# A streaming-encoder block with 32 experts: fillers placed around the routing, the tail in a planned order

## The chip, the cores and the metric

The kernel runs on one core of a Trainium2 chip. The metric is the time of one execution in microseconds (us), as a median over runs; one execution was profiled as well. The engines are named as in the profile: PE (TensorE, its weight loads PEld), DVE (VectorE), ACT (ScalarE), POOL (GpSimd) and SP, which issues most DMAs. Each engine takes its instructions in the order in which they are written.

## What is computed

For 1024 tokens of 1024 numbers, all in fp32:

```python
h = rmsnorm(x, g_mix); z = h @ w_in
x = x + concat(conv_branch(z), lru_branch(z)) @ w_out
hf = rmsnorm(x, g_ffn)
eid, gate = hier_route(hf)        # top 1 of 4 groups, then top 2 of its 8 experts
x = x + sum over the 2 chosen experts of gate * ((silu(hf @ w1[e]) * (hf @ w3[e])) @ w2[e])
e = rmsnorm(p @ w_ple, g_ple_proj)                  # p: 1024 x 256
pg = sigmoid(rmsnorm(x, g_ple) @ w_ple_gate)        # w_ple_gate: 1024 x 1024
out = rmsnorm(x + pg * e, g_final)
```

w1 and w3 are 1024 x 512 for each of 32 experts, w2 is 512 x 1024.

## The kernel before

Every fp32 matrix product is made of three fast passes on PE: each operand is split into a high part (`split_hi`, L235, a copy on ACT) and a low part (`split_lo`, L238, a subtraction on DVE, for some tiles on POOL), and high x high, high x low and low x high are summed in PSUM (`mmr`, L244). Tokens are worked in NT = 8 tiles of 128 rows.

**Front.** The code up to the routing is written as small generators (`c_...`) that a list planner, the class `Flow`, puts in order: each step names its engine, a cost and a lag, takes buffers from counted pools ("s": 36 slots of 128 x 1024) and waits for marks; among the steps that could start soonest the one of lowest rank goes first. The order that comes out is the order of the instructions, and the tile framework adds the semaphores. `c_mix` adds the mixer's output for a tile and makes hf, which goes to DRAM (hf_d); `c_router` makes the logits; `c_route` runs twice (tiles 0 to 4, then 5 to 7) and chooses experts with some 60 small DVE steps, rank matmuls (rk) and table matmuls (stab, L1083); `c_tables` reads the table into toki (the token of each row of an expert), dsti and gat. `c_ple` makes p @ w_ple for the first NPG = 5 tiles as filler work for PE, and keeps or stores (e_d) its result. `c_usplit` splits the first unit of expert weights.

**Experts.** A unit is 1 MB of one expert's weights, loaded as two slots: four units of w1/w3 (`up`) and two of w2 (`down`) for each expert, 192 in all; the list `units` puts the next expert's first two ahead of an expert's down units. Loads run AHEAD = 13 units before their use, splits SL = 2 units before. Behind the routing come the first gather of token rows (`gather`, L1349, an indirect DMA on POOL, index toki), the branch for experts with more than 128 tokens (`overflow`, L1423, not taken here) and then the loop over units. An expert's product goes silu and multiplication (`act_mul`, L1383 and L1384), transposes (hTp), a split, the down product (tile ey), a scaling by the gate (ys, L1526) and a scatter into y_d (L1354).

**Tail.** From `mctx.close()` on the framework's own scheduler orders the instructions. p for the last tiles is transposed and split, w_ple is split, `ple(i)` makes tiles 5 to 7. `load_wg` and `split_wg` bring w_ple_gate; five of its eight low parts are made on POOL (WGP). For each tile `post_norm` adds the two rows of y_d (yy) that the experts gave (L1630), squares, takes the root (`rs_of`, L287, pow on POOL), multiplies by it and g_ple (L1637) and transposes (xgT); `post_mm` makes the 48 gate matmuls (pg, for some tiles in the buffer named ey); `post_out` makes sigmoid (L1663), product with e (L1664), sum (L1665), square (L1666), root, and the last product with g_final (L1672), and stores. The last tile does this in two halves of 512 columns.

## Time and profile before

| | |
|---|---|
| median of 3 runs | 1087.73 us (1086.04 to 1088.53) |
| the profiled execution | 1087.43 us, span 1085.7 us, mean granted PE clock 0.984 |
| busy in the span | PE 1021.4 (94%), DVE 931.0 (86%), PEld 838.6 (77%), ACT 727.3 (67%), POOL 281.9 (26%) |
| DMA | 281.49 MB, mean 259 GB/s |

The span is the time from the first to the last recorded instruction or transfer; 1.7 us of the execution's time lie around it. In a timeline a row is start, duration, engine, line, operation and tiles; the bracket at its end is the idle time of the engine in front of it and what ended that. The granted clock is a share of PE's 2.4 GHz; 0.5 is 1.2 GHz.

### The profile page before, as it was taken

How to read it: one execution, taken by the hardware profiler on the slowest of the kernel's cores; microseconds unless marked ns; L12 is line 12 of the kernel's file. 1: busy time of each engine (PE TensorE's matmuls, PEld its weight loads, DVE VectorE, ACT ScalarE, POOL GpSimd, SP SyncE). 2: the span in 40 equal slices, each digit the busy share in tenths (PEclk: the TensorE clock that was granted, in tenths of full speed). 3: DMA queues.
4: the chain of work that ended last, by engine and by line, in shares of the span. 5: the costliest groups of instructions: out<-in, count | busy, mean ns of one | idle time of the engine just before them, and what ended most of it. 6: DMA issues, size and time to landing. Idle time of an engine off the chain costs nothing. (4 is left out here: it accounts for less than half of the span.)

```text
span 1085.7 us, 14177 instructions
## 1 busy us (share of the span) xinstructions
PE 1021.4 (94%) x4839; PEld 838.6 (77%) x4840; DVE 931.0 (86%) x1109; ACT 727.3 (67%) x932; POOL 281.9 (26%) x235
## 2 busy tenths in 40 slices
PE   4999999979999799999999999999999999867995
PEld 4887768758888688888888888888888888655884
DVE  5999999999556699999999999999999999669863
ACT  5447878772333688888888888888787888643331
POOL 6459576631210210111111111111010100033110
PEclk9999999999999899999999999999999999979998
DMA  9310002243326889999999999999999999477511
GB/s 270 99 39 20 19 20 78 96 155 118 117 97 207 311 315 405 400 403 401 381 395 391 381 402 385 388 392 385 382 385 382 385 379 394 154 275 290 174 40 58
DMA packets 101070, 281.49 MB, mean 259 GB/s; under 512 B 16849, under 2 KB 34945, under 8 KB 100993
## 3 DMA queue, kind: packets, MB, share of 16 engines
q1 hardware_dynamic: 89216, 255.79, 63.2%
q0 software_dynamic: 10592, 21.01, 5.2%
q10 hardware_dynamic: 1184, 3.75, 0.9%
q8 instruction: 39, 0.64, 0.2%
q14 instruction: 39, 0.31, 0.1%
HBM read 265.28 MB, written 31.98 MB: 274 GB/s over the span
## 5 line engine op out<-in xcount | busy, mean ns | idle before, releaser
L1349 POOL DMA_INDIRECT xg<-hf_d,toki x32 | 43.8, 1370 | 361.0 <-PE xgT L295 348.6
L549 DVE SCALAR_TENSOR_TENSOR fir<-u,V,fir 128x512 f32<-128x512 f32 (+20 forms) x180 | 133.2, 743 | 5.0
L235 ACT ACTIVATE xTh<-xgT 128x512 fp32r<-128x512 f32 x80 | 47.1, 598 | 77.3 <-PE xgT L295 77.3
L584 POOL TENSOR_TENSOR acc<-fpr,acc 128x512 f32<-128x512 f32 x60 | 86.2, 1437 | 40.6 <-ACT fpr L574 37.6
L1354 POOL DMA_INDIRECT y_d<-ys,dsti x32 | 39.1, 1220 | 147.9 <-ACT ys L1526 147.9
L287 POOL TENSOR_TENSOR rs<-ms,mhalf 128x1 f32<-128x1 f32 x32 | 23.2, 727 | 155.2 <-DVE ms L281 155.2
L238 DVE TENSOR_TENSOR xTl<-xgT,xTh 128x512 fp32r<-128x512 f32 x80 | 54.4, 686 | 6.8 <-ACT xTh L235 6.8
L244 PE MATMUL zvg<-hTh,whi 128*128 128x512 f32 (+1 forms) x144 | 56.7, 394 | 0.0
L244 PE MATMUL zvg<-hTh,wlo 128*128 128x512 f32 (+1 forms) x144 | 53.2, 369 | 0.0
L244 PE MATMUL zvg<-hTl,whi 128*128 128x512 f32 (+1 forms) x144 | 53.0, 368 | 0.0
L574 ACT ACTIVATE fpr<-u,V 128x512 f32<-128x512 f32 x60 | 41.9, 717 | 15.4 <-POOL acc L584 15.3
L295 PE MATMUL xgT<-ident,xg 128*128 128x128 f32 x256 | 38.8, 276 | 7.0 <-DVEq L1423 7.0
L295 PEld LDWEIGHTS xgT<-ident,xg 128*128 128x128 f32 x256 | 32.2, 142 | 14.9 <-issue 7.1
L1526 ACT ACTIVATE ys<-ey,gat 128x1024 f32<-128x1024 f32 x32 | 35.4, 1107 | 7.1 <-PE ey L244 7.1
L244 PE MATMUL wo<-wohi,lnyhl 128*128 128x512 f32 x128 | 39.4, 404 | 0.7 <-DVE lnyhl L238 0.7
L238 POOL TENSOR_TENSOR wlo<-wraw,whi 128x1024 fp32r<-128x1024 f32 x14 | 34.3, 2453 | 20.2 <-ACT whi L235 20.2
L1383 ACT ACTIVATE silu<-eab 128x512 f32<-128x512 f32 x32 | 19.2, 599 | 29.0 <-PE eab L244 29.0
L855 ACT ACTIVATE hf<-xre 128x1024 f32<-128x1024 f32 x8 | 8.5, 1058 | 42.0 <-DVE xre L843 33.4
L244 PE MATMUL pg<-wglo,xTh 128*128 128x512 f32 x96 | 32.0, 401 | 3.6 <-POOL wglo L238 2.3
L244 PE MATMUL pg<-wghi,xTl 128*128 128x512 f32 x96 | 31.7, 398 | 1.5 <-DVE xTl L238 1.5
L244 PE MATMUL pg<-wghi,xTh 128*128 128x512 f32 x96 | 32.4, 404 | 0.2 <-ACT xTh L235 0.2
L244 PEld LDWEIGHTS zvg<-hTl,whi 128*128 128x128 f32 x144 | 27.7, 192 | 5.8 <-issue 1.7
(3324 smaller groups left out, 3514.3 us busy)
## 6 DMA issues: line engine op xcount, KB each, us to landing
wraw<-in_w_in_dram SPq DMA_DIRECT2D x16, 512.0 KB, 5.1
yy<-y_d SPq DMA_DIRECT2D x16, 512.0 KB, 5.1
xin<-in_x_dram SPq DMA_DIRECT2D x8, 512.0 KB, 7.1
woraw<-in_w_out_dram SPq DMA_DIRECT2D x8, 512.0 KB, 3.7
xre<-in_x_dram SPq DMA_DIRECT2D x8, 512.0 KB, 4.1
hf_d<-hf POOLq DMA_DIRECT2D x8, 512.0 KB, 5.2
x2r<-x_d SPq DMA_DIRECT2D x8, 512.0 KB, 8.0
wgraw<-in_w_ple_gate_dram SPq DMA_DIRECT2D x8, 512.0 KB, 6.1
```

What stands on the lines that cost most here:

```text
L235: act.activation(r_(hi), src, AF.Copy)
L238: (eng or dve).tensor_tensor(out=r_(lo), in0=src, in1=hi, op=ALU.subtract)
L244: pe.matmul(out=o, lhsT=r_(l), rhs=r_(r), start=start, stop=stop)
L287: pool.tensor_tensor(out=rs, in0=ms, in1=mhalf[:, 0:1], op=ALU.pow)
L295: pe.transpose(out=t[:, k * P:(k + 1) * P], in_=src[:, off + k * P:off + (k + 1) * P], identity=ident)
L549: dve.scalar_tensor_tensor(f[:, a0 - t0:512], u[c][:, a0 - s:t1 - s], tap(c, s), f[:, a0 - t0:512], op0=ALU.mult, op1=ALU.add)
L574: act.activation(pr, u[c][:, 512 - s:1024 - s], AF.Copy, scale=tap(c, s))
L584: pool.tensor_tensor(out=a[:, 512:1024], in0=fprs.pop((c, s)), in1=a[:, 512:1024], op=ALU.add)
L1349: return pool.indirect_dma_start(out=dst, out_offset=None, in_=hf_d, in_offset=bass.IndirectOffsetOnAxis(ap=idx, axis=0), bounds_check=S - ...
L1354: return pool.indirect_dma_start(out=y_d, out_offset=bass.IndirectOffsetOnAxis(ap=idx, axis=0), in_=src, in_offset=None, bounds_check=2 * ...
L1383: act.activation(s_, w[:, 0:512], AF.Silu)
L1526: i = act.activation(ys, yw.pop(e), AF.Copy, scale=gat[:, e:e + 1])
```

## The change

It has three parts. At the routing, NPG is 4 instead of 5, the third and fourth ple tile wait for the marks "rk" and "slots" inside the routing, five units are loaded early instead of seven and a sixth right behind the first gather, the high parts of units 0 and 1 are made in the front, and the count for the branch is made ahead of the low parts. `c_mix` takes the mean of squares on POOL. In the tail, the last two units leave the loop and everything behind them is planned by a second `Flow`; w_ple_gate's raw blocks, p and half of w_ple come in during the last units; w_ple_gate is multiplied by g_ple when it is split, so that the raw sum is transposed and its root goes into the sigmoid's scale (rsx). The last tile's columns are cut into 512, 256 and 256, and its root is taken with ACT's Sqrt and DVE's reciprocal, with a small Sqrt (`c_table`) placed ahead of it. Removed with the old tail are `ple`, `e_load`, `split_wg`, `post_load`, `load_y`, `post_norm`, `post_mm` and `post_out`.

```diff
-EARLY = (3, 4, 5, 6, 7, 8, 9)
-PN0 = 6
-NPG = 5
-WGP = (1, 2, 3, 4, 5)
-PLU = 0
-PLW = 0
-WG0 = 2
-WG1 = 5
+EARLY = 5
+MORE = 6
+NPG = 4
+OFF2 = {}
+RK2 = {"pT": -30, "wp": -29, "wg": 0, "e": 12, "ple": -5, "xrs": 2}
...
@@ c_mix @@
-        yield go("DVE", 0.15)
-        ms = ms_of(ss, D)
-        yield go("POOL", 0.55)
-        rs = rs_of(ms)
+        yield go("POOL", 0.85)
+        rs = rs_of(ms_of(ss, D, pool))
...
+            order(load(x2_d[rows(i), :], xt), hfd[0], True)
...
@@ c_ple @@
+        if i == 3:
+            yield on("rk")
...
+            if i >= 2 and k == 1:
+                yield on("rk" if i == 2 else "slots")
...
+    def c_usplit(s):
+        yield on(("unit", s))
         yield get("s", 4)
         for j in range(2):
             yield go("ACT", 1.05)
             hi, lo = slot("ehi"), slot("elo")
...
+            split_hi(hi, raws[s][j])
+            his.setdefault(s, []).append((hi, lo))
...
@@ behind fl.run() @@
+    def early_lo(s, j):
+        split_lo(his[s][j][1], raws[s][j], his[s][j][0])
+        if j == 1:
+            raws.pop(s)
...
     g0 = gather(xg[0], toki[:, 0:1])
     pool.memset(gmark, 0.0)
     xg.append(bcp.tile([P, D], F32, name="xg1", tag="b"))
     pool.memset(xg[1], 0.0)
+    dve.tensor_reduce(cmx, cnt_f, op=ALU.max, axis=AX.X)
+    dve.tensor_copy(cmi, cmx)
+    for s in range(EARLY, MORE):
+        load_unit(s)
     for n, i in enumerate(ers):
         d = load(e_d[rows(i), :], ers[i])
         if n == 0:
             order(d, g0, True)
     ers.clear()
-    for s in range(len(EARLY), AHEAD):
-        load_unit(s, g0 if s == len(EARLY) else None)
-    dve.tensor_reduce(cmx, cnt_f, op=ALU.max, axis=AX.X)
-    dve.tensor_copy(cmi, cmx)
+    for s in range(MORE, AHEAD):
+        load_unit(s)
+    early_lo(0, 0)
+    early_lo(0, 1)
+    overflow()
+    early_lo(1, 0)
+    for j in range(1, NXG):
+        gather(xg[j], toki[:, j:j + 1])
+    xTs = {0: gather_T(xg[0])}
+    early_lo(1, 1)
...
@@ the loop over units @@
+    for s, (e, g) in enumerate(units[:-2]):
+        past = s + AHEAD - len(units)
+        if past == 0:
+            pt = p_load(1)
+        elif past == 1:
+            pw = {k: wp_load(k) for k in range(2)}
+        elif past > 2 and len(wgr) < 8:
+            load_wg(len(wgr))
...
+        if past in (8, 9):
+            k = past - 8
+            t = p_tr(pt, k)
             o = slot("phl")
             split_hi(o[:, 0:512], t)
             split_lo(o[:, 512:1024], t, o[:, 0:512])
-            pl[0][j, k], pl[1][j, k] = o[:, 0:512], o[:, 512:1024]
-    for k in range(2):
+            pl[0][1, k], pl[1][1, k] = o[:, 0:512], o[:, 512:1024]
+        elif past == 10:
+            k = 0
+            hi, lo = slot("wphi"), slot("wplo")
+            split_hi(hi, pw[k])
+            split_lo(lo, pw[k], hi)
+            pl[2][k] = hi, lo
...
+    def c_last():
+        e = NE - 1
+        yield get("m2")
+        yield go("ACT", 0.75, set="silu")
+        w = abw.pop(e)
+        s_ = m2("silu")
+        act.activation(s_, w[:, 0:512], AF.Silu)
+        yield go("DVE", 0.69)
+        dve.tensor_tensor(out=s_, in0=w[:, 512:1024], in1=s_, op=ALU.mult)
+        yield put("wp")
+        yield get("tp")
+        yield go("PE", 0.45, lag=0.35)
+        t = act_tr(s_)
+        yield put("m2")
+        yield get("m2", 2)
+        hi, lo = m2("hhi"), m2("hlo")
+        yield go("ACT", 0.6)
+        split_hi(hi, t)
+        yield go("DVE", 0.69)
+        split_lo(lo, t, hi)
+        yield put("tp")
+        yield get("yp")
+        w = None
+        for j in range(4):
+            yield go("PE", 6 * MM, lag=0.35 if j == 3 else 0.0)
+            w = w or ytile()
+            y_mm(w, (hi, lo), j, his[len(units) - 2 + j // 2][j % 2])
+            if j == 3:
+                yield put("m2", 2)
+            yield put("s", 2)
+        yield get("m4")
+        yl = m4("ys")
+        yield ("fork", -90, c_half(w, yl))
+        yield go("ACT", 0.6)
+        act.activation(yl[:, 0:512], w[:, 0:512], AF.Copy, scale=gat[:, e:e + 1])
+        yield on("ys1")
+        yield put("yp")
+        yield go("POOL", 1.1, lag=4.5)
+        put_rows(yl, e)
+        yield put("m4")
+        yield mark("sc")
+    def c_half(w, ys):
+        yield go("DVE", 0.69)
+        dve.tensor_scalar(ys[:, 512:1024], w[:, 512:1024], gat[:, NE - 1:NE], None, op0=ALU.mult)
+        yield mark("ys1")
...
+    def c_wps():
+        yield get("s", 2)
+        yield go("ACT", 1.05)
         hi, lo = slot("wphi"), slot("wplo")
-        split_hi(hi, pw[k])
-        split_lo(lo, pw[k], hi)
-        pl[2][k] = hi, lo
-    esq = slot("esq")
-    xs, es_, ei, yys, xTp, pgw = {}, {}, {}, {}, {}, {}
-    def ple(i):
-        w = wtile("ple") if i % 3 < 2 else ytile()
-        ple_mm(w, i, pl)
+        split_hi(hi, pw[1])
+        yield go("DVE", 1.22)
+        split_lo(lo, pw[1], hi)
+        pl[2][1] = hi, lo
+        yield put("s")
+        yield mark("pw")
...
+    def c_ple2(i):
+        yield get("wp")
+        w = None
+        for k in range(2):
+            if k:
+                yield on("pw")
+            for si in range(3):
+                yield go("PE", 2 * MM, lag=0.35 if k and si == 2 else 0.0)
+                w = w or wtile("ple")
+                ple_mm(w, i, pl, [(k, si)])
+        yield get("s")
+        es_[i] = slot("er")
+        yield ("fork", -1, c_esq(i, w))
+        yield on("gp")
+        yield go("DVE", 1.22)
+        dve.tensor_tensor(out=es_[i], in0=w, in1=gpb, op=ALU.mult)
+        yield on(("eq", i))
+        yield put("wp")
+        yield mark(("e", i))
...
+    def c_wg(k):
+        yield get("s", 2)
+        yield go("ACT", 1.05)
         hi, lo = slot("wghi"), slot("wglo")
-        split_hi(hi, raw)
-        split_lo(lo, raw, hi, pool if k in WGP else dve)
-        wg[k] = (hi, lo)
-    def post_load(i):
+        act.activation(r_(hi), wgr[k], AF.Copy, scale=vec("g_ple", k))
+        yield go("DVE", 1.22, port=True)
+        dve.scalar_tensor_tensor(r_(lo), wgr[k], vec("g_ple", k), hi, op0=ALU.mult, op1=ALU.subtract)
+        yield put("s")
+        wgs[k] = (hi, lo)
+        yield mark(("wg", k))
...
+    def c_y(i):
+        yield on("sc")
+        if i >= 2:
+            yield on(("xt", i - 2))
+        if i:
+            yield on(("yl", i - 1))
+        yield get("s", 2)
+        ys[i] = slot("y0"), slot("y1")
+        cuts = (0, 512, D) if i == 0 else (0, D)
+        for c, (a, b) in enumerate(zip(cuts, cuts[1:])):
+            f = (b - a) / D
+            for k in range(2):
+                yield go("SP", 1.35 * f, lag=0.0)
+                q = load(ys[i][k][:, a:b], y_d[k * S + i * P:k * S + (i + 1) * P, a:b])
+                for sc in scs:
+                    order(q, sc, True)
+            yield ("fork", c - 45 if i == 0 else 5, c_add(i, c, a, b))
+        yield mark(("yl", i))
...
+    def c_xt(i):
+        yield on(("xh", i, 0))
+        if i:
+            yield on(("xt", i - 1))
+        yield get("a", 2)
+        xT[i] = aslot("xTh"), aslot("xTl")
+        for q in range(2):
+            yield on(("x", i) if q else ("xh", i, 0))
+            yield get("tp")
+            yield go("PE", 0.45, lag=0.35)
+            t = ttile("x2T")
+            transposes(t, xs[i], off=q * 512)
+            yield ("fork", -40, c_xs(i, q, t))
+        yield mark(("xt", i))
+    def c_xs(i, q, t):
+        qs = slice(q * 512, (q + 1) * 512)
+        yield go("ACT", 0.6)
+        split_hi(xT[i][0][:, qs], t)
+        yield go("DVE", 0.69)
+        split_lo(xT[i][1][:, qs], t, xT[i][0][:, qs])
+        yield put("tp")
+        yield mark(("xT", i, q))
...
+    def c_pg(i, n):
+        last = i == NT - 1
+        cuts = ((0, 512), (512, 768), (768, 1024)) if last else ((0, 1024),)
+        if i:
+            yield on(("pgd", i - 1))
+        yield get(psum(n))
+        w = None
+        ss = sm("ss5", 3) if last else sm("ss5")
+        for c, (a, b) in enumerate(cuts):
             for k in range(8):
-                hi, lo = wg[k]
+                yield on(("xT", i, k // 4))
+                yield on(("wg", k))
+                yield go("PE", 6 * MM * (b - a) / 1024, lag=0.35 if k == 7 else 0.0)
+                w = w or ptile(n)
+                hi, lo = wgs[k]
                 ks = slice(k * P, (k + 1) * P)
...
+                xh, xl = xT[i]
+                for si, (l_, rr) in enumerate(((xh[:, ks], hi), (xh[:, ks], lo), (xl[:, ks], hi))):
+                    for o in range(a, b, 512):
+                        e = min(o + 512, b)
+                        mmr(w[:, o:e], l_, rr[:, o:e], k == 0 and si == 0, k == 7 and si == 2)
+            if c == len(cuts) - 1:
+                yield mark(("pgd", i))
+                yield put("a", 2)
+            yield ("fork", 20 + i, c_out(i, n, c, len(cuts), a, b, w, ss))
...
+        sg, xt, e = sgs[i], xs[i], es_[i]
+        yield go("ACT", 0.17 + 0.9 * f, set="sig")
+        act.activation(sg[:, cs], w[:, cs], AF.Sigmoid, scale=rsx[:, i:i + 1])
+        if c == nc_ - 1:
+            yield put(psum(n))
+        if nc_ > 1 and c == nc_ - 1:
+            yield ("fork", 0, c_table())
+        yield go("DVE", 0.14 + 1.08 * f, port=True)
+        dve.scalar_tensor_tensor(sg[:, cs], sg[:, cs], rse[:, i:i + 1], e[:, cs], op0=ALU.mult, op1=ALU.mult)
+        yield go("DVE", 0.14 + 1.08 * f, port=True)
+        dve.tensor_tensor(out=xt[:, cs], in0=xt[:, cs], in1=sg[:, cs], op=ALU.add)
+        yield go("ACT", 0.36 + 0.9 * f)
+        act.activation(sg[:, cs], xt[:, cs], AF.Square, accum_out=ss[:, c:c + 1])
...
+        if nc_ > 1:
+            yield go("DVE", 0.2)
+            s1 = sm("ss6")
+            dve.tensor_reduce(s1, ss, op=ALU.add, axis=AX.X)
+            yield go("ACT", 0.22, set="sqrt")
+            act.activation(s1, s1, AF.Sqrt, scale=1.0 / D, bias=epst[:, 0:1])
+            yield go("DVE", 0.2)
+            dve.reciprocal(s1, s1)
+            yield ("fork", -1, c_end(xt, s1))
+            yield go("DVE", 0.4)
+            dve.tensor_scalar(xt[:, 512:D], xt[:, 512:D], s1, None, op0=ALU.mult)
+            yield go("SP", 0.7, lag=2.6)
+            load(out[0][rows(i), 512:D], xt[:, 512:D])
+            return
...
+    def c_table():
+        yield go("ACT", 0.22, set="sqrt")
+        act.activation(sm("sd"), epst, AF.Sqrt)
+    def c_end(xt, rs):
+        yield go("ACT", 0.6)
+        act.activation(xt[:, 0:512], xt[:, 0:512], AF.Copy, scale=rs)
+        act.dma_start(out=out[0][rows(NT - 1), 0:512], in_=xt[:, 0:512])
...
+    fl.add(-90, c_last())
+    fl.add(-99, c_vec(gpb, A["g_ple_proj"], "gp"))
+    fl.add(-80, c_wps())
+    for k in range(8):
+        fl.add(RK2["wg"] + k, c_wg(k))
+    for i in range(NPG):
+        fl.add(RK2["e"] + i, c_e(i))
     for i in range(NPG, NT):
-        ple(i)
-        if i == PN0:
-            post_norm(0)
-    for i in range(8):
-        split_wg(i)
+        fl.add(RK2["ple"] + i, c_ple2(i))
+    fl.add(-10, c_vec(gfin, A["g_final"].unsqueeze(0), "gfin"))
     for i in range(NT):
...
+        fl.add(-60 + i, c_x2(i))
+        fl.add(-61 + i, c_y(i))
+        fl.add(-50 + i, c_xt(i))
+        fl.add(RK2["xrs"] + i, c_xrs(i))
+        fl.add(10 + i, c_pg(i, i))
+    fl.add(0, c_free([("e", i) for i in range(NPG, NT)], 6))
+    fl.run()
+    mctx.close()
```

`c_e`, `c_x2` and `c_vec` load the stored e, the stored x and the two gain vectors; `c_add` adds the two y rows (on DVE), `c_esq` and `c_xrs` square on ACT and take the root on POOL; tiles before the last end as before, with the pow on POOL.

## Rows read from the trace of the kernel before

**Rows 1.** Windows: PE, PEld, DVE, ACT, POOL busy (count); PEclk, DMA share, GB/s.

```profile
366.30:374.50 8.20, 1.76 (x8) 1.57 (x8) 4.15 (x8) 5.23 (x7) 4.35 (x5) 0.59 0.64 199
...
500.00:600.00 100.00, 100.00 (x475) 82.64 (x474) 92.52 (x91) 82.22 (x96) 15.55 (x12) 1.00 1.01 391
...
947.90:969.80 21.90, 11.94 (x45) 9.41 (x44) 11.21 (x14) 10.08 (x16) 4.19 (x6) 0.81 0.80 303
969.80:993.40 23.60, 16.36 (x61) 11.44 (x60) 21.51 (x17) 11.70 (x15) 16.57 (x7) 0.88 0.67 260
993.40:1074.40 81.00, 80.97 (x380) 67.21 (x380) 57.57 (x66) 27.05 (x46) 9.38 (x12) 1.00 0.32 117
1074.40:1085.70 11.30, 0.00 (x0) 0.00 (x0) 3.17 (x6) 1.32 (x3) 0.55 (x1) 0.65 0.12 46
```

**Rows 2.** Timeline around the routing: PE, then DVE, then POOL (start, duration).

```profile
365.31 0.44 PE L1083 MATMUL stab<-vv,R 128*128 128x128 f32 x3
372.74 1.94 PE L295 MATMUL xgT<-ident,xg 128*128 128x128 f32 x8 [6.98 <-DVEq L1423]
...
362.54 0.55 DVE L1079 TENSOR_TENSOR R<-iot,ranks 128x384 fp32r<-128x384 f32 x1
...
366.27 1.12 POOL L1349 DMA_INDIRECT xg<-hf_d,toki  x1 [11.07 <-DVE gat L1102]
```

**Rows 3.** Issues of the stores of e_d, by tile, 340 to 400 us.

```profile
L241 SPq DMA_DIRECT2D e_d<-er x5: 319/319/382, 355.7 to 373.0; - x5
```

**Rows 4.** Timeline of the last units: ACT, then DVE, then PE.

```profile
930.81 1.06 ACT L235 ACTIVATE ehi__9235<-eraw__8940 128x1024 fp32r<-128x1024 f32 x1
933.63 1.12 ACT L1526 ACTIVATE ys<-ey,gat 128x1024 f32<-128x1024 f32 x1 [1.76 <-PE ey L244]
...
939.70 0.69 DVE L1384 TENSOR_TENSOR silu<-eab,silu 128x512 f32<-128x512 f32 x1 [0.48 <-ACT silu L1383]
...
941.79 0.72 PE L244 MATMUL ey<-ehi__9235,hhi 128*128 128x512 f32 x2 [0.25 <-ACT hhi L235]
...
946.92 0.62 PE L244 MATMUL ey<-ehi__9264,hlo 128*128 128x512 f32 x2
```

**Rows 5.** Timeline behind the last down product: POOL, SP, DVE, PE; yy's landing.

```profile
948.98 0.97 POOL L1354 DMA_INDIRECT y_d<-ys,dsti  x1 [12.98 <-ACT ys L1526]
...
956.26 0.80 SPq L1622 DMA_DIRECT2D yy<-y_d  x2
...
962.12 2.47 DVE L1630 TENSOR_TENSOR x2r<-x2r,yy 128x1024 f32<-128x1024 f32 x2
...
968.02 1.97 PE L295 MATMUL xgT<-ident,n 128*128 128x128 f32 x8 [7.76 <-DVE ms L281]
...
DMA to landing us min/median/max: 3.6/8.4/8.8
```

**Rows 6.** A window behind a rest of PE, columns as in rows 1.

```profile
950.20:955.00 4.80, 4.80 (x14) 3.85 (x15) 2.32 (x2) 0.88 (x1) 0.00 (x0) 0.64 0.90 324
```

**Rows 7.** Chain of waits, in order of time: one piece of gate matmuls.

```profile
1055.56 18.84 PE pg L244 x83
```

**Rows 8.** Timeline of DVE: a split beside POOL's splits.

```profile
969.08 3.18 DVE L238 TENSOR_TENSOR wglo<-wgraw,wghi 128x1024 fp32r<-128x1024 f32 x1
```

**Rows 9.** ACT's table load; the last root's chain; SP's waits; stores' landing.

```profile
991.21 1.28 ACT L1663 ACT_TABLE_LOAD   x1
992.50 1.02 ACT L1663 ACTIVATE sgp<-pg 128x1024 f32<-128x1024 f32 x1
...
1074.42 0.61 ACT sgp L1663
...
1079.14 0.66 DVEq L1732
...
SPq L241 <- DVE x2r L1672: 51.5, 6, 11.8
...
DMA to landing us min/median/max: 2.0/2.0/2.6
```

More of the change, by code (lines that the diff above doesn't have):

```diff
@@ L1338, in _body @@
         fl.add(62 + i, c_ple(i))
-    fl.add(80, c_usplit())
+    for s in range(SL):
+        fl.add(80 + s, c_usplit(s))
     mctx = ExitStack()
@@ L1491, in _body @@
     pool.tensor_tensor(out=rse[:, 0:NPG], in0=ms[:, 0:NPG], in1=mhalf[:, 0:1].broadcast_to([P, NPG]), op=ALU.pow)
-    overflow()
-    for j in range(1, NXG):
-        gather(xg[j], toki[:, j:j + 1])
     abw, yw, hTs, hTt = {}, {}, {}, {}
@@ new lines, in c_esq, with c_e @@
+    def c_esq(i, w):
+        ss = sm("ss3")
+        yield get("m4")
+        yield go("ACT", 1.25)
+        act.activation(m4("esq"), w, AF.Square, accum_out=ss)
+        yield put("m4")
+        yield mark(("eq", i))
+        yield go("DVE", 0.15)
+        ms = ms_of(ss, D)
+        yield go("POOL", 0.55)
+        rs_of(ms, rse[:, i:i + 1])
+    def c_e(i):
+        yield on("sc")
+        if i:
+            yield on(("e", i - 1))
+        if i >= 2:
+            yield on(("pgd", i - 2))
+        yield get("s")
+        yield go("SP", 1.35, lag=2.6)
@@ new lines, in c_xs, with c_xrs @@
+    def c_xs(i, q, t):
[6 more added lines that the diff above has]
+        yield mark(("xT", i, q))
+    def c_xrs(i):
+        yield on(("xT", i, 1))
+        yield get("m4")
+        yield go("ACT", 1.25)
+        ss = sm("ss4")
+        act.activation(m4("xsq"), xs[i], AF.Square, accum_out=ss)
+        yield put("m4")
+        yield go("DVE", 0.15)
+        ms = ms_of(ss, D)
+        yield go("POOL", 0.55)
+        rs_of(ms, rsx[:, i:i + 1])
+        yield mark(("rsx", i))
```

269 lines of the change are left out of this document (116 added, 153 removed).

## The prediction

> **What bounds the kernel now.** I read the windows of busy time first. In the expert stage TensorE (PE) is busy for every microsecond of a window, at full clock, though the sixteen DMA engines are full too [rows 1]: a change of its edges cannot shorten its middle. PE is loose in four places of the same view: 8.2 us at 366.3 with 1.76 us of work, 21.9 us at 947.9 with 11.94, 23.6 us at 969.8 with 16.36, and the 11.3 us after the last matmul. The 81.0 us in between (993.4 to 1074.4) are solid PE. So the change can win at the hand-over from routing to experts, in the 45 us from the last expert to the second gate tile, and after the last matmul. The timelines, the waits and the chain of waits price each place.
>
> **Routing, term A.** The rank matmuls (stab) are the last PE work before the token table. Their second operand R is ready at 362.54 + 0.55 = 363.09, but the last three stab matmuls run at 365.31 and end at 365.75, because PE takes its queue in order and ple fillers stand ahead of them [rows 2]. The gather of expert 0 then starts at 366.27. The change holds a filler and a half back behind the marks "rk" and "slots" and drops a fifth ple tile (12 matmuls, 2.7 us of PE). With nothing ahead, stab ends near 363.6 and the gather starts near 364.2: 2.1 us earlier. Does it arrive? PE's transposes wait until 372.74, and the store of a kept ple tile, which waits for the gather, leaves SP at 373.0 [rows 2, 3]: so the gather lands near 372.6, 6.3 us after its start, and PE starts with it. The count for the branch is now made right behind the table, so the branch should not be late. Below zero the bound is about -3 (also the rank product unblocked earlier), above it 0, if the transfers queued before the gather set its landing. I take -2.0. The split of unit 1, moved ahead of the branch, is worth nothing by itself: behind the first transposes PE waits for no split. Its cover is unit 0's matmuls, and without them it would cost two splits, some 2.4 us. The mean of squares moved from DVE to POOL lengthens a chain off PE and costs nothing while POOL idles. Units 5 to 12 load after routing instead of 7 to 12: one unit less is ahead of a loop that holds 13, which I price at nothing.
>
> **The last units, term B.** Here the change puts work ahead of the last root. The transposes and splits of p and one split of w_ple move from behind the last down product into units 187 to 189. ACT and DVE run in order. Today ACT starts the split of unit 190 at 930.81 and then idles 1.76 us until the unit before it ends on PE (ys at 933.63) [rows 4]. After the change a p split stands ahead, which needs a transpose that PE gives only after that same unit: about 934.1. From there ACT's starts follow at 0.5 (p), 0.95, 1.0 (ys), 0.95, 0.5, 2 x 0.95 and 0.95 (w_ple): silu at 940.8. DVE follows the second half of unit 190 (937.6) with 1.14 + 0.6 + 2 x 1.14 + 1.14 and reaches the silu product at 942.8, not 939.70: +3.1 us (start distances estimated from the 1.06 us and 1.23 us durations of [rows 4, 5]). The first down matmul thus moves from 941.79 to 944.9, and fillers put ahead of it make it 945.3. I keep +2 to +6 for the range. In exchange PE has ple matmuls to do during the wait.
>
> **From the last down product to the first gate matmul, term C.** Today: last ey matmul over at 947.54, scatter on POOL at 948.98, y loads issued at 956.26, sums at 962.12, transposes at 968.02 behind a wait of 7.76 us, gate matmuls at 969.8 [rows 1, 4, 5]. The change cuts the chain's links: ys is made in two halves on two engines (about 0.5 saved), y is loaded and added in halves, square, mean, power and the product with g_ple leave the path (g_ple goes into w_ple_gate, the root into the sigmoid's scale). After: down product over at 951.05, scatter at 952.0, and 7.28 us behind it, as now, the loads: 959.3. The PE rest in B may drop the clock: the stretch of 4.8 us at 950.2 had 14 matmuls at a granted clock of 0.64 (mostly the lower, 1.2 GHz level) where full speed needs 3.2 us [rows 6]; half of that 1.6 is 0.8, making 960.1. The second load issues 0.35 later; a 256 KB half lands in 2.0 us (a store of that size, the nearest low row) to 3.6 us (the fastest 512 KB y load [rows 5, 9]); with 2.8 it is 963.25. Two half sums (0.69 each): 964.6. Four transposes at the low clock, half of the 1.97 us for eight: 965.6. The split 0.7: gate matmuls start at 966.3, against 969.8. B and C together: **-3.5 us**, with bounds -6.5 and +2.
>
> The fourth ple tile costs 2.7 us of PE here, beside waiting: four tiles are 48 x 0.227 = 10.9 us, and some 17 us lie open between 939.6 and 964.6 besides the 5.5 us of down product. Without that cover it would cost its 2.7.
>
> **Gate stage, term D.** Today 104.6 us from 969.8 to 1074.4. One matmul is 18.84 / 83 = 0.227 us [rows 7]. The solid 81.0 us hold six tiles and 46 matmuls of another, 334 x 0.227 = 75.8, leaving 5.2 for 48 transposes: 0.87 a tile. Pure work is 384 x 0.227 + 7 x 0.87 = 93.2. The 11.4 us of loss all lie before 993.4: the low clock, and waits for the low parts of w_ple_gate, whose split took DVE 3.18 us beside POOL's five [rows 8]. The change makes those splits early, with none on POOL, since the raw blocks are loaded within the last units. I keep 1.6 for the clock, 1.0 for small waits, and 0.6 for the last tile's 256-column cuts: 48 of them cost at least half of 0.227 each, at most the 0.147 of a 128-column stab matmul (0.44 for three [rows 2]), so 0 to +1.6. That is 96.4: **-8.2 us**, bounds -10.2 and -4.
>
> **The last root, term E.** Today 1074.42 to 1079.80: 5.38 us [rows 9]. After: sigmoid of 256 columns 0.40, then on ACT the table load for sqrt (1.28, as at 991.21) with its 0.2 dummy. Beside it run two DVE steps of 0.45, ready 0.5 earlier. Then square 0.5 with its accumulator read, sum 0.17, sqrt 0.2, reciprocal 0.17, last product 0.6, and hops 0.2: 3.8 us. **-1.6**, bounds -2.2 and 0. The table load is the one price open here. In the trace the load took 1.28 us from 991.21 and the sigmoid began at 992.50, neither with idle time in front of it, so a switch costs 1.3 [rows 9].
>
> The Trainium skill (ScalarE: Activation LUTs, What ACT_TABLE_LOAD costs) speaks against the step: it adds a drain of about 1380 ns to the load's 1283 ns for every switch. By that E would be about -0.2 and the time 1.4 us longer. The trace agrees with the load and shows no drain.
>
> **Sum.** -2.0 - 3.5 - 8.2 - 1.6 = -15.3. The profiled execution took 1087.43 with a span of 1085.7, 1.7 around it: span 1070.4, time 1072.1. It lies 0.3 under the median of 1087.73, so the forecast for a median is **1072.4 us**.
>
> **Rivals.** *The gather stays where it is.* For it: the DMA engines are 0.64 full in the 8.2 us at 366.3 [rows 1], and the landing may be the drain of what was queued before. Against: two units less are queued. A is 0: 1074.4. *DVE becomes the bound at the start of the gate stage.* Between 942.8 and 966 DVE has eight splits of w_ple_gate (1.28 each), one of w_ple, four ple products, the last root's halves and the sums, about 21 of 23 us. A sum whose y is late holds every split queued behind it; four held splits are 5 us. For it: static order. Against: the raw blocks are there from 940. D is then about -3.2: 1077.4. *The other side: SP's queue.* SP stood 51.5 us in six waits for finished output rows [rows 9]. If y and e loads stand behind an output store in the planned order, each of six tiles waits for its sum on PE. The time is no longer better from 15.3 / 6 = 2.6 us a tile; with 4 us a tile it is 1096. Against: two y tiles are loaded ahead, and today's order with the same waits kept PE solid for 81 us. *It does not do what it says:* the fold shortens only the first tile's chain, since later tiles already hide theirs; that is in the sum.
>
> **Chances.** Forecast 0.60; gather unmoved 0.15; DVE bound 0.17; SP queue 0.05; several of these losses at once, ending within 0.2%, 0.03. Its own errors (B +2 to +6, C, D) take the forecast from 1066 to 1078; the two smaller rivals with part of them reach 1081; that is the range, **1066 to 1081**. About 0.2% (2.2 us) is what a measurement here can tell from no change. Faster 0.92, same 0.03, slower 0.05.
>
> **What would show it.** Right: the gather starts near 364.2 and transposes near 370.7; the silu product of the last expert comes later against its last up unit than now (3 us); y loads are issued some 8 us behind the last down matmul; the gate stage takes 96 to 97 us with PE solid from its second tile; the last steps 3.8 us. Wrong: gate matmuls waiting for wglo or for a y sum; the down product at the low clock; any wait of PE per tile; the sigmoids in the way of the splits.

## The result and the profile after

The changed kernel takes 1076.65 us (median of 4 runs, 1076.09 to 1077.72), the kernel before 1087.34 (4 runs): a ratio of 0.9903, 95% interval 0.9886 to 0.9920. It is faster by 10.7 us. The forecast was 1072.4 with a range of 1066 to 1081, so sign and range hold and the point is 4.3 us too low. The profiled execution took 1076.09 with a span of 1074.4.

Windows of the kernel after, columns as in [rows 1]:

```profile
363.60:372.90 9.30, 1.57 (x8) 0.98 (x7) 3.45 (x9) 3.42 (x4) 3.16 (x4) 0.77 0.76 235
...
939.90:952.70 12.80, 10.66 (x48) 8.44 (x48) 12.10 (x13) 10.50 (x14) 1.56 (x1) 1.00 0.42 166
952.70:967.60 14.90, 9.06 (x40) 6.75 (x38) 12.14 (x17) 6.35 (x10) 5.76 (x4) 0.83 0.45 156
967.60:973.80 6.20, 6.20 (x19) 4.87 (x18) 4.01 (x5) 1.63 (x3) 0.55 (x1) 0.58 1.02 409
973.80:1066.40 92.60, 91.07 (x449) 75.87 (x447) 56.83 (x70) 34.37 (x57) 9.58 (x14) 1.00 0.37 137
1066.40:1074.40 8.00, 0.00 (x0) 0.00 (x0) 2.05 (x6) 3.28 (x7) 0.00 (x0) 0.63 0.18 66
```

PE still rests at the hand-over to the experts, 9.3 us with 1.57 of work, where [rows 1] had 8.2 with 1.76. The two loose stretches after the last expert have shrunk: DVE is now the fullest engine there (12.10 of 12.8 us, 12.14 of 14.9). The gate stage begins with 6.2 us at a mean clock of 0.58 (mostly 1.2 GHz); then come 92.6 us that PE nearly fills.

Timeline of the kernel after around the routing (SP, POOL, PE), to be held against [rows 2, 3]:

```profile
357.89 5.97 SPq L236 DMA_DIRECT2D e_d<-er  x3
363.95 0.38 SPq L236 DMA_DIRECT2D eraw__3169<-in_w_dram  x1
364.43 0.73 SPq L236 DMA_DIRECT2D eraw__3171<-in_w_dram  x1
...
364.27 1.14 POOL L1343 DMA_INDIRECT xg<-hf_d,toki  x1 [9.21 <-DVE gat L1097]
...
373.05 1.94 PE L290 MATMUL xgT<-ident,xg 128*128 128x128 f32 x8 [7.88 <-DMA xg<-hf_d,toki]
```

The gather starts at 364.27 as forecast, 2.0 us earlier, but PE gets its rows 8.78 us later instead of 6.47. Two loads of 512 KB (unit 5) are issued within 0.4 us of it.

Timeline of the kernel after from the last experts to the gate stage (DVE, PE, ACT, POOL, SP), against [rows 4, 5]:

```profile
942.75 0.69 DVE L1610 TENSOR_TENSOR silu<-eab,silu 128x512 f32<-128x512 f32 x1
...
947.13 0.61 PE L239 MATMUL ey<-ehi__9223,hhi 128*128 128x512 f32 x2
952.11 0.62 PE L239 MATMUL ey<-ehi__9262,hlo 128*128 128x512 f32 x2
...
949.35 4.27 ACT L1722 ACTIVATE wghi<-wgraw,V 128x1024 fp32r<-128x1024 f32 x4
953.51 0.67 ACT L1636 ACTIVATE ys<-ey,gat 128x512 f32<-128x512 f32 x1
...
954.22 0.75 DVE L1646 TENSOR_SCALAR ys<-ey,gat 128x512 f32<-128x512 f32 x1 [0.98 <-ACT ys L1636]
...
955.26 1.80 POOL L1348 DMA_INDIRECT y_d<-ys,dsti  x1 [3.97 <-DVE ys L1646]
...
959.34 2.69 SPq L236 DMA_DIRECT2D y<-y_d  x6
...
961.84 1.22 DVE L1686 TENSOR_TENSOR er<-ple,gp 128x1024 f32<-128x1024 f32 x1 [0.71 <-ACT esq L1695]
962.98 0.14 DVE L276 TENSOR_SCALAR ms<-ss 128x1 f32<-128x1 f32 x1
963.04 1.41 DVE L1763 TENSOR_TENSOR x2r<-x2r,y 128x512 f32<-128x512 f32 x2
...
964.50 1.11 PE L290 MATMUL x2T<-ident,x2r 128*128 128x128 f32 x4 [3.93 <-DVE x2r L1763]
966.80 1.12 PE L290 MATMUL x2T<-ident,x2r 128*128 128x128 f32 x4 [1.18 <-DVE x2r L1763]
967.57 1.20 PE L239 MATMUL pg<-wghi,xTh 128*128 128x512 f32 x2
```

The first gate matmul has moved from 969.82 to 967.57. The first sum on DVE has no idle time in front of it: it starts when the product of the last ple tile is done. And the two halves of ys, meant to run side by side, run one after the other: DVE waits 0.98 us for ACT's half. Both write one tile.

The last root of the kernel after (timeline of ACT and SP; then PE's waits from 1000 us on), against [rows 9]:

```profile
1066.80 1.28 ACT L1893 ACT_TABLE_LOAD   x1
1068.09 0.20 ACT L1893 ACTIVATE sd<-epst 128x1 f32<-128x1 f32 x1
1068.20 0.40 ACT L1853 ACTIVATE sgp<-x2r 128x256 f32<-128x256 f32 x1
...
1069.78 0.72 ACT L1897 ACTIVATE x2r<-x2r,ss 128x512 f32<-128x512 f32 x1 [0.23 <-DVE ss L1873]
1070.53 0.34 ACTq L1898 DMA_DIRECT2D out_dram<-x2r  x1
...
1070.29 0.33 SPq L236 DMA_DIRECT2D out_dram<-x2r  x1
...
PE pg L239 <- ACT sgp L1843: 1.4, 2, 0.8
```

Summed up: gather to the loop +0.3; last units up to the first gate matmul -2.6 (the loop starts 0.3 later, and is 0.7 longer); gate stage 98.7 instead of 104.6, -5.9; from the last matmul to the last product -1.2, from there to the end of the span -2.0. Together -11.3, the difference of the spans (before rounding). Which piece of the change won the 5.9 us of the gate stage (the splits made early, none of them on POOL, or the folding of g_ple) was not tried by itself.

### The profile page after: what moved, and what is told of

It is laid out like the page before. It is cut to its first block, busy times and chain, and to the rows that moved or that the text cites. A ratio compares the mean times of both kernels' runs of the same rounds, so it can differ in the third digit from the quotient of the medians.

```text
span 1074.4 us, 14195 instructions
## 1 busy us (share of the span) xinstructions
PE 1020.9 (95%) x4855; PEld 838.9 (78%) x4856; DVE 921.0 (86%) x1104; ACT 728.6 (68%) x936; POOL 266.3 (25%) x239
## 4 chain that ended last, share of the span: by engine, by line
PE 75%; DVE 16%; issue 3%; ACT 2%; DMA 2%; POOL 1%; SPq 0%; DVEq 0%; POOLq 0%; ACTq 0%
PE eab L239 32%; PE ey L239 19%; DVE fir L544 8%; PE wo L239 7%; PE pg L239 6%; PE xgT L290 3%; PE zvg L239 1%; PE hTp L290 1%; PE lgt L884 1%; DVE xr L609 1%; PE ple L239 1%; DMA xg<-hf_d,toki 1%; PE x2Tp L290 1%; PE x2T L290 1%; PE zgate L626 1%
## 5 line engine op out<-in xcount | busy, mean ns | idle before, releaser
L230 ACT ACTIVATE xTh<-xgT 128x512 fp32r<-128x512 f32 x64 | 38.2, 599 | 72.0 <-PE xgT L290 72.0
L233 DVE TENSOR_TENSOR xTl<-xgT,xTh 128x512 fp32r<-128x512 f32 x64 | 43.9, 688 | 7.6 <-ACT xTh L230 7.6
L239 PE MATMUL pg<-wghi,xTh 128*128 128x512 f32 (+1 forms) x104 | 34.5, 395 | 1.4 <-ACT sgp L1843 1.4
L239 PE MATMUL pg<-wglo,xTh 128*128 128x512 f32 (+1 forms) x104 | 33.3, 383 | 0.0
L239 PE MATMUL pg<-wghi,xTl 128*128 128x512 f32 (+1 forms) x104 | 33.2, 382 | 0.0
L239 PEld LDWEIGHTS zvg<-hTh,whi 128*128 128x128 f32 x144 | 27.8, 193 | 5.8 <-PE zgate L626 1.0
L239 PEld LDWEIGHTS zvg<-hTh,wlo 128*128 128x128 f32 x144 | 27.7, 193 | 4.6
```

The costliest lines, as they stand in the source:

```text
L230: act.activation(r_(hi), src, AF.Copy)
L233: (eng or dve).tensor_tensor(out=r_(lo), in0=src, in1=hi, op=ALU.subtract)
L239: pe.matmul(out=o, lhsT=r_(l), rhs=r_(r), start=start, stop=stop)
```

## The experiments

Every profile has its own small shift ahead of the routing: the second operand R of the last rank matmuls was ready between 362.31 and 365.26 us in the runs of the changed kernel and its variants. So stages are compared from their own anchors below. The control, a repeat of the changed kernel, took 1076.41 us (1074.66 to 1078.04), ratio 0.9890 (0.9873 to 0.9906). Three runs share its chip: p loaded earlier, fewer fillers, and the PSUM tiles. The three runs of the routing and the first trial of p's splits ran on another chip, where the kernel before took 1089.33 us, and the last ple product, PE kept busy, the old root and the five edits on a third (kernel before 1088.12 us, as beside the control); these are compared by their ratios to the kernel before. The intervals of fewer fillers, the PSUM tiles, PE kept busy, the last ple product and the old root overlap with the control's: there the stage is the evidence, and the time alone would not be.

**Control.** No edit.

> The changed kernel as it is, on the chip on which the next three run, so that these can be set against it: 1076.6 us within 1 us, transposes of expert 0 some 8.8 us behind the start of the gather, first gate matmul near 967.6, last matmul to the end of the span as in the first profile within 0.3 us. If the gather's landing or the first gate matmul differ by more than 1 us from the first profile, single profiles of the other runs can't carry differences of that size.

Transposes came 9.28 us behind the gather. The first gate matmul stood at 969.93, 1.57 of it from the later R; last matmul to the end of the span 8.1 us in both. As they stand, the first gate matmuls are 2.4 us apart, more than the 1 us set above; counted from R they differ by 0.8 us. From a nearer anchor they agree better: from the last up matmul to the issue of y it is 19.32 and 19.18 us.

**The loads beside the gather.**

```diff
-MORE = 6
+MORE = 5
```

> Only the place of unit 5's two loads (512 KB each) is changed: they go behind the stores of the kept ple tiles, and with these behind the gather. Theory 1 (the gather lands when what is queued on the DMA engines beside it has drained): at the rate of 401 to 410 GB/s of that stretch 1.05 MB less is 2.6 us less, so the gather still starts near 364.3, PE's first transposes of expert 0 move from 373.05 to about 370.7, and the time falls by about 2 us to 1074.5. Theory 2 (the gather takes its 8.7 us here for a reason of its own): transposes stay at 373.0, time 1076.6 within 1 us.

Timeline of this run, POOL and PE:

```profile
363.83 1.14 POOL L1343 DMA_INDIRECT xg<-hf_d,toki  x1 [9.23 <-DVE gat L1097]
...
368.87 1.94 PE L290 MATMUL xgT<-ident,xg 128*128 128x128 f32 x8 [4.13 <-DMA xg<-hf_d,toki]
```

5.04 us from start to transposes instead of 8.78: theory 2 falls, and theory 1 has the direction, but 3.7 us is more than its 2.6. The time is 1073.11, ratio 0.9852 (0.9836 to 0.9868). Not all of the 3.7 us arrives: at the far end DVE then waits 2.28 us for the broadcast of g_ple_proj, which stands in SP's queue behind the eight blocks of w_ple_gate (0.66 us in the changed kernel):

```profile
944.93 1.23 DVE L1686 TENSOR_TENSOR er<-ple,gp 128x1024 f32<-128x1024 f32 x1 [2.28 <-DMA gp<-in_g_ple_proj_dram]
```

**All stores of ple tiles behind the gather, too.**

```diff
-        if n == 0:
-            order(d, g0, True)
+        order(d, g0, True)
```

> As before, and all four stores of kept ple tiles wait for the gather, not one of them. Theory 1: only the store of the last normed rows and the last x rows stand beside the gather; it takes at most the 6.3 us of the kernel before, so transposes at 370.5 or earlier and a time of 1074 or less. If the loads of unit 5 alone were the cause, this run gives the same as the one without them; if the three stores share it, it is another 1 to 2 us earlier. Theory 2: transposes at 373.0 still.

This edit turned out to change nothing: three of the four tiles are stored as soon as they are done, earlier in the code, and only the last one goes through this loop. So the run repeats the one before: 4.62 us, time 1073.65, ratio 0.9856 (0.9840 to 0.9873). As the kernels are the same, the two also show how far single profiles can differ: from the last up matmul to the first down matmul 7.14 us before, 8.68 here, where PE's granted clock was 0.55 in the 3.0 us from 939.2 (1.00 there before). A window of the kernel after and the issue of its third store say more:

```profile
362.50:363.50 1.00, 0.78 (x7) 0.60 (x5) 0.89 (x5) 1.00 (x1) 0.00 (x0) 1.00 0.05 16
...
L236 SPq DMA_DIRECT2D e_d<-er x1: 320/320/320, 363.5 to 363.5; - x1
```

The DMA engines stand nearly idle (share 0.05) in the microsecond before 363.5: the first two stores have landed. The third is issued only at 363.5, 0.8 us ahead of the gather, and moves beside it. But it does so without unit 5 too (issued at 363.1 and 364.1 in the last two runs, 0.7 us ahead of the gather), and there the gather takes 5.04 and 4.62 us. So unit 5's place is the cause of the difference; what that store adds to the 5 us was not tried.

**Fillers not spaced.**

```diff
-        if i == 3:
-            yield on("rk")
...
-            if i >= 2 and k == 1:
-                yield on("rk" if i == 2 else "slots")
```

> The waits of the fillers for the marks of the rank product and the slots are taken out, the rest is as in the changed kernel: fillers stand ahead of the stab matmuls again, and the gather starts at about 366.3 instead of 364.3. Theory 1 (queued transfers set the landing): these drain at the same time, so transposes stay near 373 and the time is unchanged (within 0.5 us). Theory 2 (a fixed 8.7 us behind the start): transposes at 375 and the time 2 us longer, 1078.6.

The expectation failed in its first step: without the marks the gather still starts 1.12 us behind R, as with them (1.13), and lands 8.89 us later. So the marks buy nothing with four ple tiles; that leaves the fifth tile's 12 matmuls as the likely source of the 2.0 us, which no run tried by themselves. PE's timeline:

```profile
373.37 1.94 PE L290 MATMUL xgT<-ident,xg 128*128 128x128 f32 x8 [9.41 <-DMA xg<-hf_d,toki]
```

The time is a miss, too: 1074.13 (1072.99 to 1076.49), ratio 0.9858 (0.9841 to 0.9874), below the changed kernel's 0.9903 (0.9886 to 0.9920), where no change or a loss was expected. The profiled execution is the slowest of the four and has the stages of the changed kernel, so what made the others faster is open. The run is also only 1.0 us above the one without unit 5 beside the gather, on the same chip: how much of those 3.7 us reaches the time is not settled.

**p's splits earlier.** Transposes of p at `past` 5 and 6, their splits at 6 and 7, w_ple's first split at 8.

```diff
-        if past in (8, 9):
-            k = past - 8
-            t = p_tr(pt, k)
+        if past in (6, 7):
+            k, t = past - 6, pT
...
+        if past in (5, 6):
+            pT = p_tr(pt, past - 5)
-        elif past == 10:
+        elif past == 8:
```

> The two transposes of p are put one unit ahead of their splits, and these splits and the first one of w_ple two units earlier than in the changed kernel. Theory (ACT's wait of 3.15 us for pT and the six operations behind it make the last silu product late): the product starts near 940.7 instead of 942.75, the first down matmul of the last expert near 944.5 instead of 947.13, and the loads of y 2 to 2.5 us earlier than 959.34; if nothing else is late, the first gate matmul moves from 967.57 by as much and the time is 1074.2. Rival (DVE has no room before the sums, so the chain is bound by DVE's splits of w_ple_gate): the product comes earlier but the first gate matmul moves by less than 1 us.

A miss by its own making, PE's timeline:

```profile
931.15 1.09 PE L1164 MATMUL pT<-ident,p_in 128*128 128x128 f32 x4 [6.64 <-DMA p_in<-in_p_dram]
```

p was issued at 919.50 and landed 11.6 us later behind the unit loads. PE stood 6.64 us, and the time was 1080.61, ratio 0.9932 (0.9910 to 0.9954).

**The same with p and w_ple loaded eight units earlier.**

```diff
-        if past == 0:
+        if past == -8:
             pt = p_load(1)
-        elif past == 1:
+        elif past == -7:
```

> As in the earlier run, the transposes of p stand one unit ahead of their splits and the splits two units earlier; but now the loads of p and w_ple are issued eight units earlier, since p landed only 11 us behind its issue there and PE stood 6.64 us for it. Theory (ACT's wait for pT makes the last silu product late): no wait of PE for p; the product starts within 1 us of the last up matmul (changed kernel 2.7 us), the first down matmul about 4.7 us behind the last up unit (changed kernel 7.1 us), the loads of y 2.4 us earlier against it, and the time 2.4 us below the control. Rival (DVE, which starts its sums only at 963.04 behind a ple product, is the bound): first gate matmul and time move by less than 1 us.

DVE's timeline: the last up matmul ends at 941.18, and

```profile
941.85 0.69 DVE L1611 TENSOR_TENSOR silu<-eab,silu 128x512 f32<-128x512 f32 x1
```

0.67 us behind it instead of 2.73, and the first down matmul 4.68 us instead of 7.11: the cause of the late product is shown. But the loop itself took 569.22 us from the first transposes to the last up matmul, 2.3 more than the 566.97 of the kernel after. The first of PE's rests in it, and the load of p on SP:

```profile
892.14 0.72 PE L239 MATMUL ey<-ehi__8777,hhi 128*128 128x512 f32 x2 [0.51 <-ACT hhi L230]
...
896.75 0.39 SPq L236 DMA_DIRECT2D p_in<-in_p_dram  x1
```

PE's four rests, 1.7 us in all, lie between 892 and 909 and end with splits and products of ACT and DVE, of raw blocks that were issued by 880, ahead of p (896.75) and w_ple (900.64). So the three earlier loads do not explain them; what made the loop longer is open. Time 1075.30, ratio 0.9888 (0.9871 to 0.9904): the gain at the end of the loop did not show in the time.

**Fewer fillers ahead of the last down product.**

```diff
-        yield go("ACT", 0.6)
+        yield go("ACT", 0.1)
         split_hi(hi, t)
-        yield go("DVE", 0.69)
+        yield go("DVE", 0.1)
         split_lo(lo, t, hi)
```

> Only the planned times of the two splits of the last silu product are lowered, so that six ple matmuls instead of twelve stand between its transposes and the down product (DVE's order behind it changes too: five low parts of w_ple_gate come ahead of the first ple product). Theory (the fillers ahead of the down product, not DVE, set its start): first down matmul at about 945.7 instead of 947.13, y loads and first gate matmul 1.2 to 1.4 us earlier, time 1.3 us below the control. Rival (the down product waits for the low part of the silu product on DVE, which stood behind a split of w_ple_gate until 946.4): PE waits in the down product instead and the gain is under 0.5 us.

The first down matmul came 5.74 us behind the last up matmul, 1.37 less; y was loaded 16.70 us behind it instead of 19.32. But the sums did not follow, DVE's timeline:

```profile
961.61 1.23 DVE L1686 TENSOR_TENSOR er<-ple,gp 128x1024 f32<-128x1024 f32 x1 [0.28 <-ACT esq L1695]
...
962.81 2.74 DVE L1763 TENSOR_TENSOR x2r<-x2r,y 128x512 f32<-128x512 f32 x4
```

y was issued at 956.42 and the four sums ran without a gap from 962.81, right behind the last ple product. Of 2.6 us the first gate matmul got 0.9. Time 1073.91, ratio 0.9873 (0.9857 to 0.9890).

**The last ple product behind the sums.**

```diff
         es_[i] = slot("er")
+        if i == NT - 1:
+            yield on(("xh", 0, 1))
         yield ("fork", -1, c_esq(i, w))
```

> The square and the product of the last ple tile are ordered behind the first gate tile's sums on ACT and DVE; in the changed kernel they stand ahead. In every run so far PE rested 3.93 us between the last ple matmul and the first transposes, whenever y was loaded. Theory (the first sum waits for that product on DVE, not for y): the rest is no longer 3.93, and the first transposes come earlier, by up to 1 us; since the second half of y lands 5.6 to 6.7 us behind its first issue, the first gate matmul gains 0.5 us at most and the time stays within 0.5 us of the control here. Rival (y's landing sets the first sum): rest and first transposes as they were.

```profile
962.73 1.42 DVE L1765 TENSOR_TENSOR x2r<-x2r,y 128x512 f32<-128x512 f32 x2 [1.39 <-DMA y<-y_d]
965.02 0.69 DVE L1765 TENSOR_TENSOR x2r<-x2r,y 128x512 f32<-128x512 f32 x1 [0.87 <-DMA y<-y_d]
966.07 0.69 DVE L1765 TENSOR_TENSOR x2r<-x2r,y 128x512 f32<-128x512 f32 x1 [0.35 <-DMA y<-y_d]
```

Now the sums wait for y (DVE's timeline): the first 3.16 us behind the issue at 959.57 instead of 3.70, the last half 6.5 us. PE's rest fell from 3.93 to 3.39 us. The first gate matmul stands at 967.58, counted from the issue of y 0.2 us sooner; the issue itself was 1.1 us later behind the last up matmul, as DVE waited 1.73 us instead of 0.66 for the broadcast of g_ple_proj. So in the changed kernel DVE's order holds the first sum by half a microsecond, and y's landing the last. Time 1075.47, ratio 0.9887 (0.9872 to 0.9902).

**PE kept busy.** Sixteen matmuls with no reader stand in PE's rest.

```diff
+    def c_warm():
+        yield on("sc")
+        yield get("yp")
+        w = None
+        for k in range(8):
+            yield go("PE", 2 * MM, lag=0.0)
+            w = w or ytile()
+            for o in (0, 512):
+                mmr(w[:, o:o + 512], pl[0][1, 0][:, 0:P], pl[2][0][0][:, o:o + 512], True, True)
+        yield put("yp")
...
+    fl.add(-2, c_warm())
```

> Sixteen matmuls whose result nobody reads are put into PE's queue behind the last ple matmul, in the 3.93 us in which PE waits for the first sum; nothing else is changed. Theory (the low clock of the first gate tile, 0.58 in the 6.2 us at 967.6, follows PE's rest in front of it): the first gate tile runs at a granted clock above 0.8, the gate stage takes 96.5 us instead of 98.3 to 98.7, and the time is 1.5 to 2 us below the control. Rival (the rest of 1.2 us between the two groups of transposes, or something other than PE's rest, sets the clock): clock and stage unchanged, time unchanged.

Windows of this run, the rest and the first gate tile:

```profile
953.40:966.80 13.40, 11.62 (x54) 8.91 (x53) 11.33 (x16) 6.00 (x10) 5.76 (x4) 1.00 0.46 146
966.80:973.00 6.20, 6.20 (x33) 5.10 (x32) 4.99 (x7) 2.23 (x4) 0.55 (x1) 1.00 1.03 410
```

33 matmuls in 6.2 us at full clock, where the changed kernel did 19 at 0.58. The gate stage took 96.24 us, 2.0 to 2.5 less than in the control and the first profile (98.29, 98.70). Time 1073.29, ratio 0.9865 (0.9849 to 0.9880), 0.0025 or some 2.7 us below the control's.

**A PSUM tile for each of the last cuts.**

```diff
-                w = w or ptile(n)
+                if last:
+                    w = ws.setdefault(c, None) or ws.__setitem__(c, ptile(n) if c == 0 else ttile("pg")) or ws[c]
+                else:
+                    w = w or ptile(n)
...
-                        mmr(w[:, o:e], l_, rr[:, o:e], k == 0 and si == 0, k == 7 and si == 2)
+                        mmr(w[:, o - z:e - z], l_, rr[:, o:e], k == 0 and si == 0, k == 7 and si == 2)
...
```

> The three column cuts of the last gate tile are summed in three PSUM tiles instead of one; nothing else is changed. Theory (PE's waits of 0.84 and 0.56 us for the sigmoid between the cuts come only from the shared tile): both waits vanish, the last matmul and the end come 1.4 us earlier, 1075.2 if the control is at 1076.6. Rival (ACT and DVE need that time for the earlier cuts anyway): PE ends 1.4 us earlier but the last root starts no more than 0.5 us earlier, since the sigmoid of the last cut waits for ACT.

PE has no wait for the sigmoid left in the gate stage, which took 96.59 us; the steps behind it kept their length. The theory holds, with a stage 1.7 us shorter than in the control instead of 1.4. Time 1073.83 (1072.86 to 1076.39), ratio 0.9869 (0.9852 to 0.9885); the profiled execution is the slowest of the four.

**The old root and the old store queue.**

```diff
-            yield go("ACT", 0.22, set="sqrt")
-            act.activation(s1, s1, AF.Sqrt, scale=1.0 / D, bias=epst[:, 0:1])
-            yield go("DVE", 0.2)
-            dve.reciprocal(s1, s1)
+            ms = ms_of(s1, D)
+            yield go("POOL", 0.55)
+            s1 = rs_of(ms)
...
-        if nc_ > 1 and c == nc_ - 1:
-            yield ("fork", 0, c_table())
...
-        act.dma_start(out=out[0][rows(NT - 1), 0:512], in_=xt[:, 0:512])
+        load(out[0][rows(NT - 1), 0:512], xt[:, 0:512])
```

> Two pieces of the last root are put back: the root comes from the power on POOL instead of the square root and reciprocal on ACT and DVE (so no table load for it), and both halves of the last output are issued by SP instead of one by ACT. Theory for the root (the gain of 1.2 us comes from the column cuts and the product with g_final taken early, not from ACT's square root): the square, which stood 0.44 us behind the table load, starts at once, the power costs 0.5 us more than square root and reciprocal, so from the last sigmoid to the end of the last product 4.1 us against 4.19, within 0.2 us. Rival (the square root on ACT is the gain): 4.9 us or more. Theory for the end (the second output queue gains 2.0 us): from the last product to the end of the span 5.9 us as in the kernel before, instead of 3.9. Rival (it does not matter which queue issues): 3.9 us within 0.3.

The chain of waits, ACT's timeline with SP's, and the windows of the last microseconds:

```profile
1065.51 0.48 ACT sgp L1843
...
1068.94 0.72 ACT L1894 ACTIVATE x2r<-x2r,rs 128x512 f32<-128x512 f32 x1 [1.44 <-POOL rs L282]
1069.69 0.81 SPq L236 DMA_DIRECT2D out_dram<-x2r  x2
...
1071.30:1072.30 1.00, 0.00 (x0) 0.00 (x0) 0.00 (x0) 0.00 (x0) 0.00 (x0) 0.50 0.61 227
1072.30:1073.30 1.00, 0.00 (x0) 0.00 (x0) 0.00 (x0) 0.00 (x0) 0.00 (x0) 0.50 0.00 0
```

From the sigmoid at 1065.51 to the end of the last product at 1069.66 it is 4.15 us, against 4.19: the square root on ACT wins nothing, as the theory had it. But from there to the end of the span (1076.3) it is 6.6 us, not 3.9. The last byte moved before 1072.3, so at least 4.0 us of the span follow it; in the changed kernel bytes still moved at 1072.5 and 1.9 us followed. Time 1078.38, ratio 0.9918 (0.9903 to 0.9933).

**Five edits together**: unit 5 behind the gather, fewer fillers, three PSUM tiles, the last ple product behind the sums, and g_ple_proj loaded right behind w_ple:

```diff
             pw = {k: wp_load(k) for k in range(2)}
+            gpb = slot("gp")
+            load(gpb, A["g_ple_proj"].broadcast_to([P, D]))
```

> Five edits at once on the changed kernel: unit 5's loads behind the gather, six ple matmuls ahead of the last down product, three PSUM tiles for the last cuts, the last ple product behind the first sums, and the broadcast of g_ple_proj loaded ahead of the blocks of w_ple_gate (DVE waited 2.28 us for it once the routing was shorter). If the parts add up (3.9 us for the gather, 1.0 for the last units, 1.7 for the cuts, 1 for the order of sums and load): 7 us below the control, 1069.5, a ratio to the kernel before of 0.983. Rival (the tail is bound by the transfers of w_ple_gate and y, so what the routing and the down product win is waited for there): no more than 4 us, 1072.5.

1067.40 us (5 runs, 1064.39 to 1068.51), ratio 0.9811 (0.9797 to 0.9824): 0.0079 or some 8.6 us below the control's, clear of both intervals. The rival falls; the gain is 1.6 us more than the sum of the parts. The profiled execution is the fastest of the five, 3.0 us below their median, so its stages show a little more than the median gained. Windows of this run, columns as before:

```profile
363.60:368.80 5.20, 0.99 (x5) 0.49 (x4) 2.70 (x5) 3.42 (x4) 3.16 (x4) 0.83 0.52 168
946.80:960.20 13.40, 9.53 (x44) 7.16 (x43) 11.58 (x16) 6.04 (x11) 4.59 (x4) 1.00 0.50 172
960.20:966.40 6.20, 6.20 (x32) 5.15 (x31) 5.76 (x8) 2.13 (x5) 2.61 (x2) 1.00 1.02 411
966.40:1054.60 88.20, 88.19 (x437) 73.76 (x435) 56.47 (x70) 34.09 (x56) 11.59 (x15) 1.00 0.38 144
```

The gather lands in 5.15 us, 3.6 less than in the first profile after. From the last up matmul to the first gate matmul it is 24.74 us, 2.8 less. The gate stage is 94.35, 4.3 less: PE's rest is 2.4 us now, and the first gate tile runs at full clock without any fillers of no use.

## Why the prediction was right in sign and 4.3 us off

**A, the routing: failed.** The step that failed is "Units 5 to 12 load after routing instead of 7 to 12 ... which I price at nothing", with the assumption that the gather keeps its 6.3 us. The gather starts 2.0 us earlier, as worked out (though without the marks as well), but unit 5's loads are issued beside it: PE gets its rows 8.8 us later with them, 5.0 and 4.6 without. The forecast -2.0 came out as +0.3, which is what the rival "the gather stays where it is" gives; its count of two units less in the queue overlooked that unit 5 is new beside the gather. In the kernel before, the first load behind the kept units was ordered behind the gather; in the change only a store is. The 3.7 us are more than these 1.05 MB need at the 391 GB/s of [rows 1] (2.7 us), and only 235 GB/s moved in that window. The Trainium skill (DMA: Bandwidth & Descriptors, Queues, rings and completion order) says that each DMA engine takes turns between its queues, packet by packet. By that the gather's own 0.52 MB would lose about as long as it takes, an estimate of 1.3 us; the runs show 3.7, so the measurement goes beyond the rule, and no run shows the turns themselves. What in the mixture slows the engines is open.

**B, the last units: mechanism right, one size off.** ACT's timeline in the kernel after:

```profile
934.08 0.60 ACT L230 ACTIVATE phl<-pT 128x512 fp32r<-128x512 f32 x1 [3.15 <-PE pT L1164]
...
940.78 0.60 ACT L1608 ACTIVATE silu<-eab 128x512 f32<-128x512 f32 x1
```

The split of p waits for its transpose until 934.08 (forecast 934.1), silu starts at 940.78 (940.8), and the product at 942.75 is the forecast 942.8. The experiment with earlier splits shows the cause: 0.67 us behind PE without ACT's wait. The fillers ahead of the down product were put at 0.4 us (944.9 to 945.3); with twelve of them it started at 947.13, and six fewer bring back 1.37 us. The clock stayed full there, so the 0.8 us kept for it were not used.

**C, down product to gate matmuls: right by two errors.** y was loaded at 959.34, forecast 959.3. The way there was different: the down product ended 1.7 us later than forecast; the scatter came 2.5 us behind it instead of 0.95, since ys's halves ran in turn and ACT had four splits of w_ple_gate ahead; and the loads came 4.1 us behind the scatter, not 7.28. The last gain fits what the gather showed: in the kernel before, transfers of w_ple_gate ran beside the scatter (0.80 of the DMA engines' time [rows 1]), now 0.45 (in the 14.9 us at 952.7). This was not tried by itself. Behind the loads, the fourth ple tile, priced at nothing for its cover, held the first sum for half a microsecond through DVE's order, and y's second half landed 6.7 us behind the first issue. So the gate stage starts at 967.57, not 966.3. Once the chain is cut elsewhere, that order is the bound: there the DVE rival stands, by another mechanism than the one it named; no gate matmul waited for a low part of w_ple_gate.

**D, the gate stage: right part, losses too small.** 98.7 us, forecast 96.4: -5.9 instead of -8.2, a miss of 2.3 us as in A. The clock was put at 1.6 us and the matmuls in PE's rest show 2.0 to 2.5. Waits were put at 1.0; they are 1.4, at a place not named, the shared PSUM tile of the last cuts, whose removal gave 1.7. With both cured the stage is 94.35: work and cuts, put at 93.2 and 0.6, were 0.6 too low. No wait per tile on SP, as held against that rival.

**E, the end: -1.2 instead of -1.6, and -2.0 that nobody forecast.** The square waits 0.44 us behind the table load. The Trainium skill's drain (ScalarE: Activation LUTs, What ACT_TABLE_LOAD costs) did not show here either: the load took 1.28 us and the dummy began 0.01 us behind it. What the forecast missed is the store: with one half on ACT's queue, the span ends 2.0 us sooner behind the last product; with both back on SP's it ends 2.7 us later. Without these 2.0 us the point would be some 6 us off instead of 4.3; that part of the agreement is luck.

## What to carry to other kernels

Beside a transfer that an engine waits for, no large loads should be issued that can wait: the two loads of the sixth unit made the first expert's gather 3.7 us longer, because they were issued within 0.4 us of it. When a chain with waits on several engines is shortened, look at what each engine's fixed order puts ahead of the next link; here six fillers, one product and one broadcast at the end of a queue each held 0.5 to 2.3 us, and the gains showed in full only together. A work item "hidden" behind another engine's rest is free only if nothing that ends the rest stands behind it.

## What the hardware showed unexpectedly

The span goes on for at least 4.0 us behind the last byte when both last stores come from SP's queue, and for 1.9 us when one comes from ACT's; no row shows what runs in that time. A load of 512 KB issued in the full expert stage (p, at 919.50) kept PE waiting until 931.15, 11.6 us later.
